# A two-layer hybrid backbone on one core: squared sums and S5 taps in four column tiles, and 14 modulation units moved from the mixers to the routing

## The chip, the cores and the metric

The kernel runs on one core of a Trainium2 chip. The core has five engines, each with its own queue of instructions that it works off strictly in order: TensorE (PE, matrix products), VectorE (DVE), ScalarE (ACT), GpSimd (POOL) and SyncE (SP, which here only issues DMA transfers). They meet through semaphores. The metric is the device time of one execution in microseconds (us), median of several.

## The reference, cut to what matters

The program has two layers. `c` gives six modulation vectors for each layer, four token mixers run on one projection, gates and one output product merge them, and a routed mixture of experts follows.

```
for layer in range(DEPTH):                        # DEPTH = 2
    mod_lat = split(silu(c) @ w_mod[layer] + b_mod[layer], 6)       # w_mod: 1024 x 6144, fp32
    mod_ctx = split(silu(c_ctx) @ w_mod[layer] + b_mod[layer], 6)
    a = modulate(rmsnorm(h, norm1_g), mod[0], mod[1])
    p = split_proj(a @ w_in[layer])
    y_a = deltanet_mixer(...)      # q = l2norm(q), k = l2norm(k): sums of squares over 64 values
    y_b = s5_mixer(...)            # state space; d_skip * u is added
    y_c = diff_attention(...)
    y_d = gla_mixer(...)
    h = h + mod[2] * merge_branches(a, (y_a, y_b, y_c, y_d), w_branch, w_gate, b_gate, w_out)
    f = modulate(rmsnorm(h, norm2_g), mod[3], mod[4])
    h = h + mod[5] * moe_ffn(f, w_router, b_router, w_e_gate, w_e_up, w_e_down)
return rmsnorm(h_lat, final_g)
```

768 tokens (256 of context, 512 latent) go through layer 0, the 512 latent ones alone are needed behind layer 1. There are 16 experts of 1024 x 512 with two chosen for each token.

## The kernel before, in words

**Order.** The code is written stage by stage, but a list scheduler sets the order in which instructions stand in each engine's queue: it simulates all of them with a cost for each and lets whichever can start go ahead. The order is fixed at build time. What the chip does with it is that every engine takes the next instruction of its queue and waits for it, even if a later one could run.

**Modulation.** `mods` (L1317) makes one unit of 256 columns: two loads `w` of 512 KB on SP from three buffers (`MB = 3`), eight products `mod` (L1330, each two passes in the trace) whose weights are two columns (`c` and `c_ctx`), put in four column tiles of the array, then four additions on DVE (L1334) that sum the tiles on top of the bias `bm`, and a store to `md` in DRAM. A layer has 24 units. Eight units of layer 0 are made in front of its first norm; the other 40 (16 of layer 0, 24 of layer 1) are taken one after another from the list `todo` by `some(n)` within layer 0's mixers: 12 ahead of the first DeltaNet pair, 14 ahead of the second, 14 behind it (`MODS = (12, 14)`).

**DeltaNet.** `dn_pair` works on two of four heads. Its squared norms `dn_n` are 12 products (24 passes) with the squared values as 128 x 128 weights and a two-column mask `blk2` as the moving side. There are four calls, two in each layer.

**S5.** `s5_tables` makes in two halves the tables of a layer: powers and products `W`, `O` on DVE and POOL, products `s_w`, and the taps `s_h` (L1088), 16 products (32 passes) in each half with 32-column weights `Bd`, all into PSUM partitions 0 to 31. The taps `H` go by DRAM (`hd`) into the table `td`. Layer 1's tables are made at the end of layer 0's mixers: they reuse the space of layer 0's S5 mixer (whose last products are `s_g`), begin with the load of `sp` (L960), and the merge stands behind them.

**Gates and merge.** The gate products `pg` of the mixers (1536 of them, split precision: `wh`, `wl` are made on ACT and by DVE or POOL at L1289 and L1290) fill PE between the mixers' own steps. The merge begins with `pb<-yh,wh`.

**Routing and experts.** `route` is a generator: up to its `yield` it makes positions (`pos`), one-hots (`hot`) and the first block's tokens; behind it the counts (`cnt`) and the order of the remaining blocks. `moe` then runs 128-token blocks: transpose `pt`, products `pg` (gate and up), transpose `ph`, products `pd` (down). Expert weights come as `raw` loads of 1 MB on SP, are split into `hi` (ACT, L2203) and `lo` (DVE or POOL, L2205).

Of the kernel before, what the change touches and what calls it, by code (L numbers as in the profile page):

```python
# [17 lines left out]
NT = 6  # L18
# [9 lines left out]
PRI = (None, None)  # L28
PRG = (None, None)
PVM = 64  # L30
MODS = (12, 14)
MB = 3
RAW = (3, 5)
RAW2 = (2, 1)
# [7 lines left out]
def const_blob():  # L42
    p = np.arange(128)
    k, i = p[:, None], p[None, :]
    same = (k // 64) == (i // 64)
    j64, i64 = (p % 64)[:, None], np.arange(64)[None, :]
    t = np.arange(512)
    inv = (np.float32(10000.0) ** (-np.arange(8, dtype=np.float32) / np.float32(8))).astype(np.float32)
    ang = np.concatenate([(t // 64).astype(np.float32)[:, None] * inv, (t % 64).astype(np.float32)[:, None] * inv], -1)
    rope = [f(ang).astype(np.float32).reshape(4, 128, 16).transpose(1, 0, 2).reshape(128, 64) for f in (np.cos, np.sin)]  # L50
    parts = dict(
        id=(k == i), id64=(j64 == i64), trif=same & (k <= i), trib=same & (k >= i), blk=same,
        cm0=(k < 64) & (i >= 0), cm1=(k >= 64) & (i >= 0),
        mskf=i64 >= j64, mskb=i64 <= j64, blk2=(k // 64) == np.arange(2)[None, :],
        cos=rope[0], sin=rope[1],
        gmf=(i >= k) * np.float32(32 ** -0.5), gmb=(i <= k) * np.float32(32 ** -0.5),
        id16=(k % 16 == np.arange(16)[None, :]) * 1.0,
        stri=(k < i), one=(k >= 0) & (i >= 0),
        tok=p[:, None] + 128 * np.arange(6)[None, :], exp=np.arange(16)[None, :] * 768 + 0 * k,
        num1=np.arange(1, 16)[None, :] + 0 * k, num16=np.arange(16)[None, :] + 0 * k,  # L60
        iota=i + 0 * k,
    )
    off, cols, c = {}, [], 0
    for n, a in parts.items():
        a = np.ascontiguousarray(a).astype(np.float32)
        off[n] = (c, a.shape[1])
        c += a.shape[1]
        cols.append(a)
    return np.concatenate(cols, 1), off

PRM = (("lre", 16), ("lim", 16), ("ldt", 16), ("bin", 256), ("ct", 512), ("dsk", 8),
       ("g1", 8), ("bm1", 16), ("cc", 16), ("bgt", 32), ("convw", 30), ("dng", 64), ("dtb", 8), ("na", 8),
       ("wg", 256), ("bg", 2), ("glag", 64), ("lv", 128), ("dag", 64), ("glub", 2), ("wr", 128), ("br", 16), ("g2c", 8))
PRO = {n: (sum(m for _, m in PRM[:i]), m) for i, (n, m) in enumerate(PRM)}
# [6 lines left out]
def lay_out(x):  # L83

    a = {n: np.asarray(x[n], dtype=np.float32) for n in x}
    o = {}
    prm = np.zeros((2, 128, NPRM), np.float32)

    def put(l, nm, v):
        c, n = PRO[nm]  # L90
        v = np.asarray(v).reshape(-1, n)
        prm[l, 0:v.shape[0], c:c + n] = v
# [8 lines left out]
    for l in range(2):  # L101
        for nm, src in (("lre", "s5_a_re"), ("lim", "s5_a_im")):
# [2 lines left out]
        put(l, "bin", np.stack([a[n][l].reshape(8, 128, 16).transpose(1, 0, 2) for n in ("s5_b_re", "s5_b_im")], 1))  # L105
        put(l, "ct", np.stack([a[n][l].reshape(2, 8, 2, 16, 64).transpose(2, 4, 0, 1, 3).reshape(128, 2, 128)
                               for n in ("s5_c_re", "s5_c_im")], 2))
        put(l, "dsk", a["s5_d"][l].reshape(8, 32).T)
# [151 lines left out]
def tcol(t):  # L260

    return 128 * t + (4 if t >= 2 else 0)
# [95 lines left out]
def dn_pair(K, l, pr, S, qT, kT, vT, o_out, need):  # L358
# [3 lines left out]
    nc, p, sm = K.nc, K.dn, K.dn_sm  # L362
    idm = K.c("id")
# [10 lines left out]
    sq = [s3([128, 772], "sq") for _ in range(2)]  # L374
    nc.scalar.activation(sq[0], qT, AF.Square)
    nc.scalar.activation(sq[1], kT, AF.Square)
    pn = K.psm("dn_n")
    pnv = pn[:, 0:24].rearrange("p (s t h) -> p s t h", s=2, t=NT)
    for s in range(2):
        for t in range(NT):  # L380
            nc.tensor.matmul(pnv[:, s, t, :], sq[s][:, tcol(t):tcol(t) + 128], K.c("blk2"), start=True, stop=True)
    n2 = sm.tile([128, 24], F32, tag="n2", name="n2")
    nc.vector.tensor_scalar(n2, pn[:, 0:24], 0.25, 1e-6, op0=OP.mult, op1=OP.add)
    rr = rsqrt_(nc, sm, n2, [128, 24], "nr")
    rq = sm.tile([128, NT, 2], F32, tag="rq", bufs=2, name="rq")
    nc.vector.tensor_scalar(rq.rearrange("p t h -> p (t h)"), rr[:, 0:12], 0.125 * 0.5, None, op0=OP.mult)
# [16 lines left out]
    for src, dst, isk in ((kT, Kt, True), (vT, Rv, False)):  # L403
        for t0, n in ((0, 4), (4, 2)):
# [4 lines left out]
            pv = pt[:, 0:n * 128].rearrange("p (a e) -> p a e", e=64)  # L409
# [11 lines left out]
    for cp in range(2):  # L421
        src = bass.AP(tensor=gd.tensor, offset=gd.offset + pr * 24 * 128 + cp * 64, ap=[[0, 64], [128, 24], [1, 64]])
# [41 lines left out]
    for c in range(31):  # L464
        n, m = 31 - c, c + 1
# [101 lines left out]
    for s0, s1 in ((0, 8), (1, 9), (8, 11), (9, 11)):  # L567
# [4 lines left out]
        pv = pb.rearrange("p (s c) -> p s c", c=128)  # L572
# [378 lines left out]
def s5_params(K, l):  # L951
# [4 lines left out]
    def t16(nm):  # L956
        return q.tile([128, 16], F32, tag=nm, name=nm)

    sp = q.tile([128, 824], F32, tag="sp", name="sp")
# [52 lines left out]
    dsk = sp[0:32, 816:824]  # L1012

    rot = q.tile([128, 2, 7, 16], F32, tag="rot", name="rot")
    wr, wi = cs, sn
# [14 lines left out]
def s5_tables(K, l, P, h, td):  # L1030
# [45 lines left out]
    for b in range(2):  # L1076
        r = slice(64 * b, 64 * b + 64)
        for c in range(2):
            G.tensor_copy(Bd[r, c, :, :, 16 * b:16 * b + 16], bb[r, c, :, H4, :])
    H = s4([32, 4, 15, 16], "H")  # L1080
    pss = [K.psmt("s5_h") for _ in range(2)]
    for g in range(4):
        a, o = g // 2, (g % 2) * 256
        for d in range(2):
            lo = 0 if d == 0 else 1
            c0 = o + (128 if d == 0 else 0)
            for c in range(2):
                nc.tensor.matmul(pss[a][0:32, c0:c0 + 128], Bd[:, c, d, g], O[d][:, c, g, lo:lo + 8].rearrange("p e c -> p (e c)"),  # L1088
                                 start=(c == 0), stop=(c == 1))
    for a in range(2):  # L1090
        pv = pss[a][0:32].rearrange("p (g s n) -> p g s n", g=2, s=2)
        Ha = H[:, 2 * a:2 * a + 2]
        nc.scalar.activation(Ha[:, :, 0:8].rearrange("p g n c -> p g (n c)"), pv[:, :, 0], AF.Copy)
        nc.scalar.activation(Ha[:, :, 8:15].rearrange("p g n c -> p g (n c)"), pv[:, :, 1, 16:128], AF.Copy)
        V.tensor_add(Ha[:, :, 7], Ha[:, :, 7], pv[:, :, 1, 0:16])
    dd = p.tile([32, 4, 16], F32, tag="dd", name="dd")
    V.tensor_mul(dd, P["dsk"][:, H4, None].to_broadcast([32, 4, 16]), K.c("id16")[0:32, None, :].to_broadcast([32, 4, 16]))
    V.tensor_add(H[:, :, 7], H[:, :, 7], dd)
    hd = K.dram.tile([32, 4, 240], F32, tag="s5h", bufs=2, name="hd")
    nc.sync.dma_start(hd[:], H.rearrange("p g n c -> p g (n c)"))  # L1100
    cz = sum(n for _, n in S5_TAB[0:4])
    for j in range(8):
        src = hd[:, :, 16 * (7 - j):16 * (7 - j) + 128].rearrange("(b c) g k -> c g b k", b=2)
# [386 lines left out]
def mixers(K, l, md, hold, tile_of, yd, gd, tds):  # L1490
# [91 lines left out]

    if l == 0:
        pm = Hold(tc, "mod1", "left")
        todo = iter([(0, u) for u in range(8, 24)] + [(1, u) for u in range(24)])

        def some(n):
            for _ in range(n):
                i, u = next(todo)
                mods(K, i, md[i], [u], pm, MB, K.psmb)  # L1590

        some(MODS[0])
# [31 lines left out]


    if l == 0:
        some(40 - MODS[0] - MODS[1])
        pm.close()

    def sink_tm(dst, c0, n):  # L1630
# [330 lines left out]
    V.tensor_add(R.tot[:, t0:t1], sel[:, 0], sel[:, 1])  # L1961


def route(K, l, lg, R):

# [385 lines left out]
def backbone(nc, tc, I, out, off):  # L2353
# [37 lines left out]
    for l in range(2):  # L2391
# [30 lines left out]
        routing = route(K, l, lg, R)  # L2422
        next(routing)
        nh = pm[0]
        hs = {}
# [46 lines left out]
```

## Time and profile before

| | |
|---|---|
| median of 3 runs | 2811.99 us (2797.94 to 2814.32) |
| profiled execution | 2812.61 us, of it 2810.6 us span on the core |
| mean granted TensorE clock | 0.908 of full speed |
| PE busy over the span | 2443.4 us (87%) |
| DVE, ACT, POOL busy | 1870.6, 1218.6, 1178.3 us (67, 43, 42%) |

The span runs from the core's first to its last instruction. Busy time is an average over stages with different limits, so the stages are looked at one by one. Layer 0's mixers lie between 118 and 945 us, its merge runs to 1110, its routing from 1110 to 1186 and its experts to about 1530. A PEclk of 1.00 is 2.4 GHz and 0.50 is 1.2 GHz.

### The profile page before, as it was taken

Reading aid. Unit: us, or ns where it says so; the run is one execution under the profiler, and the core shown is the slowest. Engines: PE = TensorE matmul, PEld = TensorE weight load, DVE = VectorE, ACT = ScalarE, POOL = GpSimd, SP = SyncE. Lnnn points to the kernel's source line nnn. Section 1 sums busy time; section 2 is a strip of 40 time slices with the busy share of each in tenths; the row PEclk is TensorE's granted clock in tenths of the full one; section 3 lists DMA queues with packets and bytes.
Section 4 is the critical chain, followed back from the end, with each engine's and each line's share of the span. In section 5 each row is a group of like instructions: output and inputs, shape, how many; then the busy total and the mean of one; then the engine's idle time right before and its main releaser. Section 6 shows DMA issues by size and latency. Waiting matters only on the chain. (4 is left out here: it accounts for less than half of the span.)

```text
span 2810.6 us, 46335 instructions
## 1 busy us (share of the span) xinstructions
PE 2443.4 (87%) x17539; PEld 1974.6 (70%) x17539; DVE 1870.6 (67%) x3515; ACT 1218.6 (43%) x1889; POOL 1178.3 (42%) x854
## 2 busy tenths in 40 slices
PE   6789998899998788599998499989998886699993
PEld 5567687777776676478887388977776665478782
DVE  5968639545659765877775744665584576787775
ACT  4121232365443322366665323244655432366672
POOL 2701205522417453466664320155343043576763
PEclk9889999999988999699999699989998598799996
DMA  7488832414322775478887553343432184588884
GB/s 295 163 260 287 263 91 74 145 58 143 113 82 95 266 228 201 178 271 307 305 306 253 209 186 116 100 130 120 113 102 62 57 263 170 196 335 298 305 309 160
DMA packets 227896, 534.95 MB, mean 190 GB/s; under 512 B 85478, under 2 KB 108230, under 8 KB 202054
## 3 DMA queue, kind: packets, MB, share of 16 engines
q1 hardware_dynamic: 216710, 510.81, 53.5%
q0 software_dynamic: 10944, 20.99, 2.1%
q8 instruction: 142, 2.33, 0.3%
q14 instruction: 100, 0.82, 0.1%
HBM read 452.33 MB, written 100.35 MB: 197 GB/s over the span
## 5 line engine op out<-in xcount | busy, mean ns | idle before, releaser
L2205 DVE TENSOR_TENSOR lo<-raw,hi 128x2048 fp32r<-128x2048 f32 x124 | 418.2, 3381 | 106.3 <-ACT hi L2203 106.1
L2203 ACT ACTIVATE hi<-raw 128x2048 fp32r<-128x2048 f32 x192 | 364.2, 1913 | 79.3 <-issue 34.8
L2205 POOL TENSOR_TENSOR lo<-raw,hi 128x2048 fp32r<-128x2048 f32 x68 | 335.9, 4941 | 142.0 <-ACT hi L2203 127.5
L1290 POOL TENSOR_TENSOR wl<-wr,wh 128x512 fp32r<-128x512 f32 x128 | 185.0, 1449 | 295.5 <-ACT wh L1289 276.2
L1301 PE MATMUL pg<-ah,wl 128*128 128x512 f32 (+1 forms) x768 | 286.4, 374 | 7.1 <-POOL wl L1290 7.1
L1299 PE MATMUL pg<-ah,wh 128*128 128x512 f32 (+1 forms) x768 | 286.8, 374 | 5.8 <-ACT wh L1289 3.7
L1300 PE MATMUL pg<-al,wh 128*128 128x512 f32 (+1 forms) x768 | 286.4, 373 | 0.0
L1300 PE MATMUL pg<-lo,xh 128*128 128x512 f32 x608 | 244.9, 403 | 13.8 <-DVE lo L2205 11.0
L1299 PE MATMUL pg<-hi,xh 128*128 128x512 f32 x608 | 243.8, 404 | 5.4 <-ACT xh L2230 4.0
L1301 PE MATMUL pg<-hi,xl 128*128 128x512 f32 x608 | 243.0, 401 | 0.0
L1289 ACT ACTIVATE wh<-wr 128x512 fp32r<-128x512 f32 (+3 forms) x208 | 147.8, 715 | 206.9 <-PE pg L1300 66.8
L1301 PEld LDWEIGHTS pg<-ah,wl 128*128 128x128 f32 x768 | 151.9, 198 | 31.1 <-POOL wl L1290 8.0
L1299 PEld LDWEIGHTS pg<-ah,wh 128*128 128x128 f32 x768 | 152.1, 198 | 28.7 <-ACT wh L1289 4.2
L1300 PEld LDWEIGHTS pg<-al,wh 128*128 128x128 f32 x768 | 152.0, 198 | 22.8 <-issue 0.2
L1300 PE MATMUL pt<-wl,ah 128*128 128x256 f32 (+1 forms) x544 | 159.0, 293 | 2.2 <-DVE wl L1290 2.2
L1299 PE MATMUL pt<-wh,ah 128*128 128x256 f32 (+1 forms) x544 | 158.4, 292 | 2.3 <-ACT zst L1578 2.3
L1301 PE MATMUL pt<-wh,al 128*128 128x256 f32 (+1 forms) x544 | 157.6, 290 | 0.0
L870 DVE TENSOR_REDUCE nm<-da_m 128x1 f32<-128x384 f32 (+1 forms) x144 | 76.2, 539 | 120.0 <-PE da_m L869 118.9
L1300 PEld LDWEIGHTS pg<-lo,xh 128*128 128x128 f32 x608 | 116.9, 192 | 42.0 <-DVE lo L2205 14.4
L1299 PEld LDWEIGHTS pg<-hi,xh 128*128 128x128 f32 x608 | 117.2, 193 | 29.9 <-ACT xh L2230 5.1
L1301 PEld LDWEIGHTS pg<-hi,xl 128*128 128x128 f32 x608 | 116.8, 192 | 23.2
L1299 PE MATMUL pd<-hi,hh 128*128 128x512 f32 x304 | 120.6, 397 | 7.3 <-ACT hh L2257 4.2
(735 smaller groups left out, 6172.1 us busy)
## 6 DMA issues: line engine op xcount, KB each, us to landing
raw<-in_w_e_gate SPq DMA_DIRECT2D x64, 1024.0 KB
raw<-in_w_e_up SPq DMA_DIRECT2D x64, 1024.0 KB
raw<-in_w_e_down SPq DMA_DIRECT2D x64, 1024.0 KB
w<-in_wm SPq DMA_DIRECT2D x80, 512.0 KB
wr<-in_w_gate SPq DMA_DIRECT2D x128, 256.0 KB
wr<-in_win SPq DMA_DIRECT2D x40, 512.0 KB
gd<-gst SPq DMA_DIRECT2D x32, 384.0 KB
g<-gd SPq DMA_DIRECT2D x32, 384.0 KB
```

The lines of the kernel that those rows point to most:

```text
L870: nc.vector.tensor_reduce(nm[:, g, m, qt:qt + 1], ps[:, 0:k1 - k0], axis=AX.X, op=OP.max, negate=True)
L1289: nc.scalar.activation(h, r, AF.Copy)
L1290: (nc.gpsimd if pool_lo else nc.vector).tensor_sub(l, r, h.bitcast(F32))
L1299: nc.tensor.matmul(out, ah, bh, start=(i == 0), stop=False)
L1300: nc.tensor.matmul(out, ah, bl, start=False, stop=False)
L1301: nc.tensor.matmul(out, al, bh, start=False, stop=(i == n - 1))
L2203: nc.scalar.activation(h, r, AF.Copy)
L2205: (nc.gpsimd if (j % 3 == 2 if pool_lo is None else pool_lo) else nc.vector).tensor_sub(l_, r, h.bitcast(F32))
```

## The change

Three parts. In the DeltaNet norms the mask becomes the weights (32 columns, `blk32`) and the squared values the moving side, in four column tiles; a copy on ACT, three transposes and one smaller DVE operation bring the sums back. In the S5 taps the four groups of a half go to four column tiles, which leaves two copies and two DVE operations where there were four and four. Of the 40 modulation units 26 stay in the mixers (12, 12 and 2) and 14 are made in `route`, called ahead of its `yield` in the first layer, with three `w` buffers of their own and two PSUM buffers `fill` of the routing's pool.

```diff
-MODS = (12, 14)
+MODS = (12, 12, 2)
...
     pn = K.psm("dn_n")
-    pnv = pn[:, 0:24].rearrange("p (s t h) -> p s t h", s=2, t=NT)
-    for s in range(2):
-        for t in range(NT):
-            nc.tensor.matmul(pnv[:, s, t, :], sq[s][:, tcol(t):tcol(t) + 128], K.c("blk2"), start=True, stop=True)
+    for x in range(3):
+        for c in range(4):
+            a = tcol(3 * (c % 2) + x)
+            nc.tensor.matmul(pn[32 * c:32 * c + 32, 128 * x:128 * x + 128], K.c("blk32"), sq[c // 2][:, a:a + 128],
+                             start=True, stop=True)
+    ns = s3([128, 384], "ns")
+    nc.scalar.activation(ns, pn[:, 0:384], AF.Copy, scale=0.25)
+    pn = K.psm("dn_n")
+    for x in range(3):
+        nc.tensor.transpose(pn[:, 128 * x:128 * x + 128], ns[:, 128 * x:128 * x + 128], idm)
     n2 = sm.tile([128, 24], F32, tag="n2", name="n2")
-    nc.vector.tensor_scalar(n2, pn[:, 0:24], 0.25, 1e-6, op0=OP.mult, op1=OP.add)
+    nc.vector.tensor_scalar(n2.rearrange("p (c x h) -> p c x h", c=4, x=3),
+                            pn[:, 0:384].rearrange("p (x c e) -> p c x e", x=3, c=4)[:, :, :, 0:2], 1e-6, None, op0=OP.add)
...
-    H = s4([32, 4, 15, 16], "H")
-    pss = [K.psmt("s5_h") for _ in range(2)]
-    for g in range(4):
-        a, o = g // 2, (g % 2) * 256
-        for d in range(2):
...
+    H = s4([128, 15, 16], "H")
+    ps = K.psmt("s5_h")
+    for d in range(2):
+        lo, c0 = d, 128 * (1 - d)
+        for c in range(2):
+            for g in range(4):
+                nc.tensor.matmul(ps[32 * g:32 * g + 32, c0:c0 + 128], Bd[:, c, d, g], O[d][:, c, g, lo:lo + 8].rearrange("p e c -> p (e c)"),
                                  start=(c == 0), stop=(c == 1))
...
-        todo = iter([(0, u) for u in range(8, 24)] + [(1, u) for u in range(24)])
+        todo = iter([(0, u) for u in range(8, 20)] + [(1, u) for u in range(14)])
...
-        some(40 - MODS[0] - MODS[1])
+        some(MODS[2])
...
     G.tensor_add(all_, pre[:, n - 1], tot[:, n - 1])
+    fill(lambda nm: pp.tile([128, 512], F32, tag="fill", bufs=2, name=nm))
     pp.close()
     p.close()
     yield
...
+        def fill(psm):
+            if l == 0:
+                pf = Hold(tc, "mod2", "left")
+                for i, u in [(0, u) for u in range(20, 24)] + [(1, u) for u in range(14, 24)]:
+                    mods(K, i, md[i], [u], pf, MB, psm)
+                pf.close()
```

What stands in the queues moves at two places. On PE, at the end of layer 0's mixers, where layer 1's tables (`s_w`, `s_h`) are made and the merge (`pb`) begins, this stood before:

```order
L910 MATMUL da_s<-st 128x512
L1058 MATMUL s_w<-cb,W 128x128 x4
L1300 MATMUL pg<-al,wh 128x256
...
L1088 MATMUL s_h<-O,Bd 32x128 x16
...
L1465 MATMUL yT<-cb,o 128x128 x6
...
L1300 MATMUL pg<-al,wh 128x512
L1301 MATMUL pg<-ah,wl 128x512
L1299 MATMUL pb<-yh,wh 128x256
```

and this stands there now:

```order
L1065 MATMUL s_w<-cb,W 128x128 x4
L1299 MATMUL pg<-ah,wh 128x512
L1300 MATMUL pg<-al,wh 128x512
L1301 MATMUL pg<-ah,wl 128x512
L1093 MATMUL s_h<-O,Bd 32x128 x8
L1465 MATMUL yT<-cb,o 128x128 x6
L1065 MATMUL s_w<-cb,W 128x128 x4
L1093 MATMUL s_h<-O,Bd 32x128 x8
L1065 MATMUL s_w<-cb,W 128x128 x12
L1093 MATMUL s_h<-O,Bd 32x128 x16
L1299 MATMUL pb<-yh,wh 128x256
```

The gate products have moved forward: ahead of the last `s_g` of layer 0 stand 1348 of them rather than 1151 (of the difference of 197, 97 are 512 columns wide and 100 are 256) and 449 products of the differential attention rather than 418; between the first `s_w` and `pb` stand 34 gate products rather than 219, and none at all behind the first `s_h`.

On PE at layer 0's routing, where `pos` begins the routing's own products and `pt` the first expert block, this stood before:

```order
L1869 MATMUL pq<-sel,lt 128x16 x2
L2004 MATMUL pos<-seltot,cb 128x96
L2007 MATMUL pos<-pre,cb 128x96
L2020 MATMUL ent<-v_12110,hot 128x2 x6
L2051 MATMUL wt<-w_12138,hot 128x1 x6
L2091 MATMUL cnt<-all,cb 128x16
L2228 MATMUL pt<-cb,x 128x128 x4
L1299 MATMUL pg<-hi,xh 128x512
```

and this stands there now:

```order
L1869 MATMUL pq<-sel,lt 128x16 x2
L1330 MATMUL mod<-w,sc 2x256 x28
L2004 MATMUL pos<-seltot,cb 128x96
L2007 MATMUL pos<-pre,cb 128x96
L1330 MATMUL mod<-w,sc 2x256 x4
L2020 MATMUL ent<-v_11818,hot 128x2 x6
L1330 MATMUL mod<-w,sc 2x256 x8
L2051 MATMUL wt<-w_11846,hot 128x1 x6
L1330 MATMUL mod<-w,sc 2x256 x72
L2229 MATMUL pt<-cb,x 128x128 x4
L2092 MATMUL cnt<-all,cb 128x16
L1299 MATMUL pg<-hi,xh 128x512
```

All 112 products of the 14 units stand ahead of the first expert block, 84 of them behind `pos`.

On SP, whose queue issues the loads at the same place, this stood before (`iota` is the routing's first load, `h1d` and `fd` its last stores):

```order
L1992 DMA iota<-in_blob 128x128
L2200 DMA raw<-in_w_e_up 128x2048
L2200 DMA raw<-in_w_e_down 128x2048
L1844 DMA h1d_86<-h 128x1024
L1890 DMA fd_87<-h 128x1024 x2
L2200 DMA raw<-in_w_e_down 128x2048
```

and this stands there now:

```order
L1992 DMA iota<-in_blob 128x128
L1325 DMA w<-in_wm 128x1024 x2
L1332 DMA bm<-in_b_mod 2x256
L1844 DMA h1d_86<-h 128x1024
L1325 DMA w<-in_wm 128x1024
L1332 DMA bm<-in_b_mod 2x256
L1890 DMA fd_87<-h 128x1024
L1325 DMA w<-in_wm 128x1024
L1890 DMA fd_87<-h 128x1024
L1325 DMA w<-in_wm 128x1024 x2
L1335 DMA md_67<-bm 2x256
```

The rest of the 28 loads `w` follows, with three `raw` loads among them; the second half of the first block's `up` weights, which stood right behind `iota`, and its second `down` load stand behind the last store of the units.

## Rows read from the trace of the kernel before

**Rows 1.** Windows of the mixers: stretch, length, busy us (instructions) per engine, PEclk, DMA, GB/s.

```profile
200.00:350.00 150.00, 139.62 (x1778) 105.09 (x1775) 112.29 (x236) 33.63 (x62) 26.43 (x19) 0.96 0.86 272
400.00:650.00 250.00, 234.00 (x2180) 194.84 (x2178) 143.53 (x300) 113.71 (x243) 97.69 (x85) 0.94 0.33 95
...
850.00:900.00 50.00, 42.30 (x304) 34.59 (x303) 50.00 (x157) 17.85 (x35) 34.01 (x28) 0.90 0.27 93
900.00:950.00 50.00, 35.95 (x181) 29.65 (x180) 35.84 (x105) 12.60 (x24) 31.91 (x54) 0.84 0.67 233
```

**Rows 2.** The modulation's products among the groups of PE in 118 to 400 us.

```profile
L1330 PE MATMUL mod<-w,sc 128*2 128x256 f32 x640 | 53.7, 411 | 22.5 <-DMA w<-in_wm 21.4 <-DVE R L939 1.0
```

**Rows 3.** Instructions of the tile `mod`: ns min/median/max, first and last start.

```profile
L1330 PE MATMUL mod<-w,sc x640: 376/378/634, 124.6 to 356.9; 128*2 128x256 f32 x160
L1334 DVE TENSOR_TENSOR bm<-mod,bm x160: 402/417/427, 130.3 to 362.0; 2x256 f32<-2x256 f32 x160
```

**Rows 4.** Instructions of the lines of the DeltaNet norms and the S5 taps.

```profile
L381 PEld LDWEIGHTS dn_n<-cb,sq x96: 186/192/238, 192.8 to 2029.0; 128*128 128x128 f32 x96
L381 PE MATMUL dn_n<-cb,sq x96: 165/251/298, 192.9 to 2029.0; 128*128 128x2 f32 x96
...
L1088 PEld LDWEIGHTS s_h<-O,Bd x128: 106/110/177, 91.7 to 921.4; 128*32 128x32 f32 x128
L1088 PE MATMUL s_h<-O,Bd x128: 272/273/422, 91.7 to 921.5; 128*32 128x128 f32 x128
```

**Rows 5.** Timeline of SP and PE, end of the mixers: start, us, instruction.

```profile
829.46 0.47 SPq L960 DMA_DIRECT2D sp<-in_prm  x1
...
918.94 2.81 PE L1088 MATMUL s_h<-O,Bd 128*32 128x128 f32 x24 [1.23 <-DVE O L1071]
948.70 0.58 PE L1299 MATMUL pb<-yh,wh 128*128 128x256 f32 x1 [2.76 <-ACT wh L1289]
```

**Rows 6.** Groups of DVE in 829 to 935 and of POOL in 829 to 945 us.

```profile
L916 DVE SCALAR_TENSOR_TENSOR pe<-pe,nlam 128x512 f32<-128x512 f32 (+1 forms) x8 | 7.5, 935 | 0.0
L1290 POOL TENSOR_TENSOR wl<-wr,wh 128x512 fp32r<-128x512 f32 x13 | 21.1, 1626 | 22.3 <-ACT wh L1289 20.0 <-issue 2.4
```

**Rows 7.** Timeline of SP at the routing.

```profile
1111.35 0.33 SPq L1992 DMA_DIRECT2D iota<-in_blob  x1
...
1124.98 1.08 SPq L1890 DMA_DIRECT2D fd<-h  x2
```

**Rows 8.** Timeline of PE at the routing.

```profile
1133.42 0.74 PE L2004 MATMUL pos<-seltot,cb 128*128 128x96 f32 x2 [15.80 <-DVE seltot L1961]
...
1151.51 1.11 PE L2228 MATMUL pt<-cb,x 128*128 128x128 f32 x4 [5.67 <-DMA x<-fd,tokfirst]
...
1174.92 0.39 PE L1301 MATMUL pg<-hi,xl 128*128 128x512 f32 x1
...
1186.01 0.77 PE L1299 MATMUL pd<-hi,hh 128*128 128x512 f32 x1 [0.82 <-DVE wtranked L2071]
```

**Rows 9.** Windows of the modulation loads, the routing and the experts; columns as in rows 1.

```profile
160.00:340.00 180.00, 169.62 (x1919) 125.46 (x1921) 137.10 (x289) 48.76 (x86) 24.11 (x19) 0.96 0.84 271
1150.00:1160.00 10.00, 2.76 (x7) 1.54 (x7) 10.00 (x5) 0.60 (x1) 10.00 (x3) 0.50 0.71 268
1240.00:1300.00 60.00, 60.00 (x284) 49.59 (x284) 42.74 (x27) 41.82 (x37) 39.84 (x16) 1.00 0.80 296
```

**Rows 10.** Timeline of DVE and of POOL at the routing.

```profile
1134.09 4.43 DVE L2039 TENSOR_TENSOR ws<-w 128x6 f32<-128x6 f32 x1
1147.98 4.27 DVE L2096 TENSOR_SCALAR over<-cnt 128x14 f32<-128x14 f32 x1
1152.17 0.15 DVE L2137 TENSOR_SCALAR c<-cnt 1x16 f32<-1x16 f32 x1
...
1133.98 4.52 POOL L2205 TENSOR_TENSOR lo<-raw,hi 128x2048 fp32r<-128x2048 f32 x1
1146.63 14.54 POOL L2205 TENSOR_TENSOR lo<-raw,hi 128x2048 fp32r<-128x2048 f32 x3
```

More of the change, by code (lines that the diff above doesn't have):

```diff
@@ L53, in const_blob @@
         cm0=(k < 64) & (i >= 0), cm1=(k >= 64) & (i >= 0),
-        mskf=i64 >= j64, mskb=i64 <= j64, blk2=(k // 64) == np.arange(2)[None, :],
+        mskf=i64 >= j64, mskb=i64 <= j64, blk32=(k // 64) == np.arange(32)[None, :],
         cos=rope[0], sin=rope[1],
@@ L69, in const_blob @@
     return np.concatenate(cols, 1), off
-PRM = (("lre", 16), ("lim", 16), ("ldt", 16), ("bin", 256), ("ct", 512), ("dsk", 8),
+PRM = (("lre", 16), ("lim", 16), ("ldt", 16), ("bin", 256), ("ct", 512), ("dsk", 2),
        ("g1", 8), ("bm1", 16), ("cc", 16), ("bgt", 32), ("convw", 30), ("dng", 64), ("dtb", 8), ("na", 8),
@@ L107, in lay_out @@
                                for n in ("s5_c_re", "s5_c_im")], 2))
-        put(l, "dsk", a["s5_d"][l].reshape(8, 32).T)
+        put(l, "dsk", a["s5_d"][l].reshape(2, 128).T)
         put(l, "g1", cm(a["norm1_g"][l]))
@@ L957, in t16 @@
         return q.tile([128, 16], F32, tag=nm, name=nm)
-    sp = q.tile([128, 824], F32, tag="sp", name="sp")
+    sp = q.tile([128, 818], F32, tag="sp", name="sp")
     nc.sync.dma_start(sp, prm(K, l, "lre", "dsk"))
@@ L1011, in s5_params @@
     ct = sp[:, 304:816].rearrange("p (d c g i) -> p d c g i", d=2, c=2, g=8)
-    dsk = sp[0:32, 816:824]
+    dsk = sp[:, 816:818]
     rot = q.tile([128, 2, 7, 16], F32, tag="rot", name="rot")
@@ L1079, in s5_tables @@
             G.tensor_copy(Bd[r, c, :, :, 16 * b:16 * b + 16], bb[r, c, :, H4, :])
-    H = s4([32, 4, 15, 16], "H")
-    pss = [K.psmt("s5_h") for _ in range(2)]
-    for g in range(4):
-        a, o = g // 2, (g % 2) * 256
-        for d in range(2):
[L1085 to L1088, printed above, removed]
-                                 start=(c == 0), stop=(c == 1))
@@ L1090, in s5_tables @@
[L1090 to L1097, printed above, removed]
@@ L1098, in s5_tables @@
-    V.tensor_add(H[:, :, 7], H[:, :, 7], dd)
-    hd = K.dram.tile([32, 4, 240], F32, tag="s5h", bufs=2, name="hd")
-    nc.sync.dma_start(hd[:], H.rearrange("p g n c -> p g (n c)"))
+    H = s4([128, 15, 16], "H")
[5 more added lines that the diff above has]
+                nc.tensor.matmul(ps[32 * g:32 * g + 32, c0:c0 + 128], Bd[:, c, d, g], O[d][:, c, g, lo:lo + 8].rearrange("p e c -> p (e c)"),
+                                 start=(c == 0), stop=(c == 1))
@@ L1101, in s5_tables @@
+    nc.scalar.activation(H[:, 0:8].rearrange("p n c -> p (n c)"), ps[:, 0:128], AF.Copy)
+    nc.scalar.activation(H[:, 8:15].rearrange("p n c -> p (n c)"), ps[:, 144:256], AF.Copy)
+    V.tensor_add(H[:, 7], H[:, 7], ps[:, 128:144])
+    V.scalar_tensor_tensor(H[:, 7], K.c("id16"), P["dsk"][:, h:h + 1], H[:, 7], op0=OP.mult, op1=OP.add)
+    hd = K.dram.tile([128, 240], F32, tag="s5h", bufs=2, name="hd")
+    nc.sync.dma_start(hd[:], H.rearrange("p n c -> p (n c)"))
     cz = sum(n for _, n in S5_TAB[0:4])
@@ L1102, in s5_tables @@
     for j in range(8):
-        src = hd[:, :, 16 * (7 - j):16 * (7 - j) + 128].rearrange("(b c) g k -> c g b k", b=2)
+        src = hd[:, 16 * (7 - j):16 * (7 - j) + 128].rearrange("(g b c) k -> c g b k", g=4, b=2)
         dst = td[16 * j:16 * j + 16, cz:cz + 1024].rearrange("c (g b k) -> c g b k", g=4, b=2)
@@ L1961, in choose, with route @@
     V.tensor_add(R.tot[:, t0:t1], sel[:, 0], sel[:, 1])
-def route(K, l, lg, R):
+def route(K, l, lg, R, fill):
     nc, tc, I = K.nc, K.tc, K.I
@@ L2421, in backbone @@
         R.ent = rk.tile([128, 2, NT - 2 * l, 4], I32, name="ent")
-        routing = route(K, l, lg, R)
+        def fill(psm):
[4 more added lines that the diff above has]
+                pf.close()
+        routing = route(K, l, lg, R, fill)
         next(routing)
```

## The prediction

> **What bounds the kernel now.** I read the windows by stage first, then the groups of the moved work, then the timelines around the two places where the queues change. In layer 0's mixers PE is busy for 139.62 of 150 us while the modulation units are made and for 234.00 of 250 behind them [rows 1], so work taken off PE there should come back, unless another chain sets the end. At the end it does: from 850 to 900 us DVE is busy for 50.00 of 50 and PE for 42.30, from 900 to 950 PE for 35.95 [rows 1]. There layer 1's S5 tables are made, from the load of `sp` at 829.46 to the last taps at 918.94 + 2.81 = 921.75, and the merge begins at 948.70 [rows 5]. Layer 0's routing is bound neither by PE nor by DMA alone: PE waits 15.80 us for `seltot` [rows 8], has 2.76 busy us of 10 at a granted clock of 0.50, the 1.2 GHz level, and DVE and POOL are both full [rows 9]. So PE has room there, DVE has little. Behind it the experts keep PE busy for 60.00 of 60 us at a clock of 1.00 [rows 9]: whatever the first block loses is lost at the end too.
>
> **The mixers, what is taken away.** The 40 units cost PE 53.7 us, and 21.4 us went in waits for their `w` loads [rows 2]. One unit is 53.7 / 40 = 1.34 us, 14 are 18.8. Of the waits I give them their share, 14/40 of 21.4 = 7 us (bounds 0 and 21). A call of the norms is 24 weight loads of 0.192 us, 4.6 us; the new weights have 32 columns like those of the taps, whose load takes 0.110 [rows 4], which gives 2.6, from which three transposes and a copy on ACT, whose result DVE waits for, take a part back: 1 us a call, 2 for layer 0 (bounds -2 and +5 for both, the old cost halved or the new steps all on the chain). In sum 18.8 + 7 + 2 = 28 us of PE time.
>
> A norm product with 2 moving columns takes 251 ns and a tap product with 128 takes 273 [rows 4], so the moving side, 64 times longer now, costs nearly nothing. A rule speaks against the change there: the Trainium skill, TensorEngine Tiling (Array Packing), Tiling Modes, says that a change of the tiling mode drains the engine. By an estimate from that rule, one product of 251 ns lost going in and one coming out, the four norm calls and four tap halves would pay 8 x 0.5 = 4 us and their gain would be gone; no row here shows a drain by itself.
>
> **The mixers, what is put in its place.** The order has moved the gates forward. Ahead of layer 0's last `s_g` stand 97 more gate products of 512 columns, 100 of 256 and 31 more of the differential attention. The experts show 284 products in 60.00 us, 0.211 us each [rows 9], so these are 97 x 0.211 + 100 x 0.106 + 31 x 0.13 = 20.5 + 10.6 + 4.0 = 35 us (the halves are estimates by width). S5's mixer then ends at -28 + 35 = +7 us. The load of `sp` follows it directly, and the tables behind it are DVE's. They can only become shorter: within them DVE has 7.5 us of the attention's `pe` and POOL 21.1 us of the gates' `wl` [rows 6], nearly all of which is done earlier now, since 34 gate products are left rather than 219. Bounds are 0 and 7.5 + 21.1 = 29; I take half, 14, because POOL is not the chain's only engine. So the merge begins at +7 - 14 = **-7 us**. PE's gates no longer cover the tables: the time that PE saved is spent waiting for taps. Range: -28 if the whole saving passes through, +7 if the tables are not shorter. The merge itself I cost at nothing; its products and loads are the same.
>
> **The routing.** The 112 `mod` products stand on PE ahead of `pt`, so the first block begins behind the last unit, at a time T. Three routes give T.
> By bytes: `iota` is at 1111.35 and the second `fd` at 1124.98 [rows 7]; `fd` waits for POOL and DVE, and on SP all but three or four of the 28 loads wait behind it. About 25 loads of 0.52 MB and three `raw` of 1.05 MB are 16 MB; at 271 GB/s, the rate in the mixers [rows 9], this is 60 us, T = 1185.
> By the units' own pace: before, 40 of them ran from 124.6 to 356.9 [rows 3], 5.8 us each with three buffers; 14 from 1111 on give 1111 + 81 = 1192.
> By PE: 14 x 1.34 = 18.8 us at a clock of 1.00, up to twice that at 0.50, which fits under the loads.
> DVE's 56 additions are 56 x 0.417 = 23 us [rows 3], put in among the routing's chain. That chain is held where POOL runs: `ws` of six columns takes 4.43 us beside a `lo` of 4.52, `over` 4.27 within the three `lo` of 14.54 [rows 10]. Additions queued behind such an operation wait with it, and their PSUM buffers are two, so PE waits then too: up to two holds, 9 us. I take **T = 1188**, bounds 1183 and 1200.
>
> On these holds the trace shows a pattern: `over`, on 128 partitions, takes 4.27 us, the copy `c` right behind it 0.15 [rows 10]. The Trainium skill, GPSIMD Engine Reference, Specifications, says that GpSimd shares its SBUF interfaces with VectorE and contends with those of its instructions that use two ports or have two SBUF inputs. By that rule the additions themselves, with one input in PSUM, would pass; the result by this rule alone would be T = 1185 and 3 us less in the sum. Rows 3 cannot decide it, their maximum of 427 ns has little of POOL beside it.
>
> From T to the first `pd`: before, from the first `pt` at 1151.51 to `pd` at 1186.01 [rows 8] were 34.5 us with waits; without them the 48 gate and up products, the transposes and the step from the last `pg` (1174.92) to `pd` (11 us, [rows 8]) come to some 17 us, 22 if the second `up` load, issued only behind the last store, is late with its split (1.05 MB are 3.9 us at 271 GB/s, and POOL's `lo` takes 4.52, [rows 10]). Taken 19: `pd` at 1188 + 19 = 1207, against 1186.01: **+21 us**, range 1183 + 17 - 1186 = +14 to 1200 + 22 - 1186 = +36. The experts pass it on in full.
>
> **Layer 1 and the taps.** Two norm calls at 1 us, and taps on the path: the last 24 passes take 2.81 us [rows 5], at best a quarter in four tiles, with two DVE operations fewer. Together -3 us, bounds -8 and +2.
>
> **The sum** is -7 + 21 - 3 = +11 us. The profiled execution took 2812.61 us, 0.6 above the median, so both give **2823 us**.
>
> **The rivals.**
> 1. *The mixers keep all that PE saves.* PE is the fullest engine there [rows 1], and if the tables shrink by the whole 29 us, the merge begins 28 us earlier or so. Against it: DVE is at 50.00 of 50 in the tables with little of the rest. With +21 at the routing and -3: 2803; with the routing's +14 as well, 2796. Only if the routing also hides its units (rival 3) is it 2780, faster by more than 1%.
> 2. *The units hold the experts back longer* (slower than before). SP is one queue: a store of `md` that waits for DVE's additions stands ahead of the next `w`, and DVE's additions stand behind the held routing operations. If each unit behind `pos` (1133.42, [rows 8]) takes the pace of before (5.8 us) plus two holds, 10.5 units end at 1133.4 + 61 + 9 = 1203, and with the late `up` load `pd` is at 1225, +39; with S5's chain at +7, the sum is +43, 2855. With the late load it passes 1% from T = 1188 on if the chain is at +7 (+7 + 24 - 3), from T = 1202 with the forecast's -7. For it: DVE is full and the queues are strict. Against it: the pace of before was set by the mixers' other work as much as by the buffers.
> 3. *The routing hides the units.* Before, PE waited 5.67 us for the first block's tokens [rows 8], and DVE's chain was held until POOL's three `lo` ended at 1161 [rows 10]; both would now run beside the units. If T is 1172 and DVE's chain is then out of the way, the routing costs +5: -7 + 5 - 3 gives 2807. Against it: 16 MB do not load by 1172 at any rate shown in rows 9.
> 4. *The tiles do not run side by side.* Norms and taps then cost as before or more: +5 on the forecast, 2828, no case of its own in the chances.
>
> **How the numbers follow.** About 1%, 28 us, is what a measurement of this kernel tells from no change (the three runs lie 16 us apart). Forecast 0.42, rival 1 0.23, rival 2 0.17, rival 3 0.18. The forecast and rival 3 lie within 1%, so does rival 1 but for its meeting with rival 3 and a larger share of waits (0.10 to 0.13); rival 2 is beyond it at nearly all its times. Faster 0.13, same 0.70, slower 0.17. For 8 in 10 the range leaves out the low end of rival 1 and the high end of rival 2: 2793 to 2850. The predicted time is the forecast's, 2823.
>
> **What would show it.** The merge's first `pb` near 942 with PE idle ahead of the taps in 830 to 920; the `sp` load a few us later than 829; the last `mod` product at 1183 to 1200 and the first `pd` at about 1207; PE full in the experts, ending some 11 us later. Wrong would be: `pb` before 925 (rival 1), a last `mod` product behind 1200 (rival 2) or before 1175 (rival 3).

## The result, and the profile after

| | before | after |
|---|---|---|
| median | 2811.77 us, 4 runs | 2849.97 us, 4 runs (2837.60 to 2856.82) |
| ratio | | 1.0141, 95% interval 1.0091 to 1.0191 |
| profiled execution, span | 2812.61, 2810.6 us | 2853.99, 2852.2 us |
| mean granted TensorE clock | 0.908 | 0.901 |

The change costs 38 us where 11 were forecast: the sign was right, the size was not, and the time lies at the very end of the range. To see what one trace is worth, each kernel was profiled a second time (the last two experiments). These are the milestones on PE in us, in all four traces:

| from, to | before | before again | after | after again | mean change | forecast |
|---|---|---|---|---|---|---|
| start to first `dn_n` | 193 | 200 | 199 | 191 | -1 | 0 |
| to the merge's first `pb` | 756 | 755 | 756 | 749 | -2 | -7 |
| to `pos` | 185 | 185 | 188 | 187 | +3 | } +21 |
| to the first `pd` | 53 | 53 | 86 | 91 | +36 | } |
| layer 0's experts, to their last `pd` | 352 | 352 | 353 | 352 | +1 | 0 |
| to layer 1's first `pb` | 706 | 695 | 699 | 699 | -1 | } -3 |
| to the last `pd` | 525 | 522 | 528 | 528 | +4 | } |

So the loss lies in one place, between `pos` and the first `pd`. I follow the prediction's steps there. The windows of the mixers and the experts after (columns as in rows 1):

```profile
200.00:350.00 150.00, 140.66 (x1760) 117.56 (x1753) 102.20 (x206) 38.69 (x71) 26.22 (x19) 0.99 0.68 202
400.00:650.00 250.00, 231.74 (x2092) 192.32 (x2091) 155.82 (x322) 109.71 (x245) 104.11 (x86) 0.91 0.32 91
850.00:900.00 50.00, 44.02 (x320) 36.71 (x318) 46.36 (x172) 16.55 (x30) 27.38 (x24) 0.93 0.27 95
900.00:950.00 50.00, 7.83 (x64) 4.26 (x64) 43.00 (x174) 5.46 (x12) 34.78 (x53) 0.51 0.51 170
```

From 900 to 950 us PE is busy for 7.83 us at the 1.2 GHz level, where it had 35.95 [rows 1]: the gates no longer cover the tables, as forecast. The group of the `mod` products in 118 to 400 us, the lines of the norms and the taps, and then (from the timelines of SP and PE) the end of the mixers:

```profile
L1330 PE MATMUL mod<-w,sc 128*2 128x256 f32 x416 | 35.8, 422 | 16.9 <-DMA w<-in_wm 11.1 <-DVE R L954 5.3 <-DVE B L473 0.3
```

```profile
L381 PEld LDWEIGHTS dn_n<-sq,cb x96: 106/110/111, 199.0 to 2089.7; 128*32 128x32 f32 x96
L381 PE MATMUL dn_n<-sq,cb x96: 272/273/298, 199.0 to 2089.8; 128*32 128x128 f32 x96
...
L1093 PE MATMUL s_h<-O,Bd x128: 272/421/424, 99.1 to 931.0; 128*32 128x128 f32 x128
```

```profile
850.15 0.42 SPq L967 DMA_DIRECT2D sp<-in_prm  x1
...
929.16 2.27 PE L1093 MATMUL s_h<-O,Bd 128*32 128x128 f32 x32
955.57 0.58 PE L1299 MATMUL pb<-yh,wh 128*128 128x256 f32 x1 [24.14 <-ACT wh L1289]
```

The units left in the mixers cost 35.8 us and 11.1 of waits, against 53.7 and 21.4 [rows 2]: 17.9 and 10.3 us less, where 18.8 and 7 were forecast. The `sp` load comes 20.7 us later than before [rows 5], the last taps some 10 us later, and `pb` 7: the tables took back two thirds of it.

PE at the routing, and SP there:

```profile
1143.41 0.74 PE L2004 MATMUL pos<-seltot,cb 128*128 128x96 f32 x2 [0.39 <-DVE seltot L1961]
...
1196.69 1.89 PE L1330 MATMUL mod<-w,sc 128*2 128x256 f32 x16 [3.83 <-DVE bm L1334]
1198.51 1.12 PE L2229 MATMUL pt<-cb,x 128*128 128x128 f32 x4
...
1215.57 0.39 PE L1301 MATMUL pg<-hi,xl 128*128 128x512 f32 x1
...
1227.87 1.11 PE L2257 MATMUL ph<-cb,hd 128*128 128x128 f32 x4 [8.98 <-DVE hd L2247]
1229.67 0.79 PE L1299 MATMUL pd<-hi,hh 128*128 128x512 f32 x1 [0.69 <-ACT hh L2258]
```

```profile
1117.69 0.33 SPq L1992 DMA_DIRECT2D iota<-in_blob  x1
...
1132.35 0.73 SPq L1890 DMA_DIRECT2D fd<-h  x1
...
1201.31 0.36 SPq L2201 DMA_DIRECT2D raw<-in_w_e_up  x1
```

The last `mod` product ends at T = 1198.6, 80.9 us behind `iota`, where the forecast has 1188 - 1111.35 = 76.7 [rows 7]. From T to the last `pg` of the first block are 17 us, but `pd` follows only 31 us behind T, because `ph` waits 8.98 us for DVE's `hd`. In the kernel before it waited 1.02:

```profile
1177.86 0.65 PE L2256 MATMUL ph<-cb,hd 128*128 128x128 f32 x4 [1.02 <-DVE hd L2246]
```

DVE and POOL around these 31 us:

```profile
1194.42 3.58 DVE L1334 TENSOR_TENSOR bm<-mod,bm 2x256 f32<-2x256 f32 x8 [6.74 <-DMA bm<-in_b_mod]
1199.17 1.77 DVE L1334 TENSOR_TENSOR bm<-mod,bm 2x256 f32<-2x256 f32 x4 [1.18 <-DMA bm<-in_b_mod]
...
1201.06 0.17 DVE L2094 COPY cnt<-cnt 128x16 f32<-128x16 f32 x1
...
1208.13 2.29 DVE L2206 TENSOR_TENSOR lo<-raw,hi 128x2048 fp32r<-128x2048 f32 x1 [0.84 <-ACT hi L2204]
...
1220.30 0.67 DVE L2246 SCALAR_TENSOR_TENSOR hd<-hd,pg 128x512 f32<-128x512 f32 x1
...
1221.40 3.55 DVE L2161 SCALAR_TENSOR_TENSOR ova<-ovb,ova 1x192 f32<-1x192 f32 x1
1224.88 0.14 DVE L2024 TENSOR_SCALAR pr<-ent 128x4 f32<-128x4 f32 x1
1224.95 2.27 DVE L2206 TENSOR_TENSOR lo<-raw,hi 128x2048 fp32r<-128x2048 f32 x1
1227.15 0.67 DVE L2247 TENSOR_TENSOR hd<-hd,pg 128x512 f32<-128x512 f32 x1
```

```profile
1212.46 19.15 POOL L2206 TENSOR_TENSOR lo<-raw,hi 128x2048 fp32r<-128x2048 f32 x2 [4.99 <-ACT hi L2204]
```

`cnt` starts the routing's chain of small DVE operations. Before, `over`, its second step, was at 1147.98 [rows 10], ahead of the first `pt`; now the chain begins 2.5 us behind T. The second half of the first block's `up` weights is loaded at 1201.31, behind the last store of the units, and its split with those of `down` puts four `lo` of 2.3 us ahead of the first `hd` and a fifth ahead of the second; `ova`, one of many rows of 0.34 us, takes 3.55 here, within the time of POOL's two `lo`, in which other rows of its form take 0.34 as well.

The last unit's products wait 3.83 us for additions of DVE, and these wait 6.74 us for a bias load `bm`, which stands on SP's one queue behind the stores `md` and loads `w` of other units. The additions themselves are not drawn out: the longest of the 160 takes 427 ns, as before [rows 3].

### The profile page after: what moved, and what is told of

The parts are those of the page before. It is cut to its first block, busy times and chain, and to the rows that moved or that the text cites. A ratio compares the mean times of both kernels' runs of the same rounds, so it can differ in the third digit from the quotient of the medians.

```text
span 2852.2 us, 46349 instructions
## 1 busy us (share of the span) xinstructions
PE 2426.7 (85%) x17551; PEld 1948.1 (68%) x17551; DVE 1872.5 (66%) x3507; ACT 1214.9 (43%) x1885; POOL 1193.8 (42%) x854
## 5 line engine op out<-in xcount | busy, mean ns | idle before, releaser
L1300 PE MATMUL pc<-al,wh 128*128 128x256 f32 (+3 forms) x352 | 123.4, 351 | 2.4 <-DVE al L1404 1.6
```

Of the source, the lines that this page charges most:

```text
L1300: nc.tensor.matmul(out, ah, bl, start=False, stop=False)
```

## The experiments

The kernel before was run beside each, and each ratio is to those runs. Two theories stood against each other at the start: that the 14 units beside the routing cost what is missing, or that the new order of the queues does, wherever the work lies.

**One part of the change alone.** The tiles alone, all 40 units left in the mixers:

```diff
-MODS = (12, 12, 2)
+MODS = (12, 14)
-        todo = iter([(0, u) for u in range(8, 20)] + [(1, u) for u in range(14)])
+        todo = iter([(0, u) for u in range(8, 24)] + [(1, u) for u in range(24)])
```

> The norms and taps in column tiles, all 40 modulation units left in the mixers. Theory 1 (all of the loss comes from the 14 moved units): 2804 to 2813 us, the first merge product within 5 us of 948.7, first pd of layer 0 within 8 us of 1186. Theory 2 (the column tiles, by the engine's change of tiling mode or by the order they bring, make the mixers longer): 2818 to 2830 us, the merge's first product at 955 or later.

2854.86 us, ratio 1.0175 (1.0136 to 1.0213). That is a loss as large as the whole change's, without a unit beside the routing. In its trace `pos` to `pd` take 53 us as before; the loss lies in layer 1, whose code is that of the changed kernel: its mixers take 724 us there and 699 in the changed kernel. The units moved alone, norms and taps as before:

> The 14 units moved to the routing, norms and taps as before. Theory 1: 2846 to 2860 us, first pd of layer 0 at 1225 to 1240. Theory 2: 2830 to 2840 us, since the mixers would keep their 7 us.

2898.60 us, 1.0333 (1.0295 to 1.0370). The parts cost 48 and 92 us, both together 38: they do not add up, so what one such run costs is not the price of its edit. The norms alone, and the taps alone:

> The kernel before with the new norms alone. Theory E (the norms' chain now passes PE's queue twice, and the transposes stand behind gate products, 18 us in the second pair of the changed kernel): the time from the first dn_n product to the n operation is 8 us or more in at least one of four calls, 2815 to 2850 us. Theory F (norms are neutral): 2800 to 2812 us.

> The kernel before with the new taps alone. Theory E: 2800 to 2812 us, the taps behind the last table operation 2 us shorter. Theory F (the taps' tiles or the order they bring cost the 48 us of both together): 2840 us or more.

2868.84 us, 1.0203 (1.0150 to 1.0256), and 2813.66 us, 1.0007 (0.9979 to 1.0036). With the taps alone the first `pd` lies 998 us behind the first `dn_n`, against 993 and 992, and nothing is lost or gained.

**The order by itself.** The kernel before without the 14 units (only their bias is loaded and stored, so their products, sums and weight loads are left out):

```diff
-                    mods(K, i, md[i], [u], pf, MB, psm)
+                    bias(K, i, md[i], u, pf)
```

> The kernel before without the 14 units (their columns are the bias alone), norms and taps as before: the mixers have the PE time back and nothing is paid for it. Theory A (PE's time in the mixers is not what ends them: waits and the clock take its place): 2800 to 2820 us. Theory B (the mixers would be faster, but the column tiles ate it in the changed kernel): 2775 to 2792 us, the merge's first product before 930.

2859.35 us, 1.0204 (1.0127 to 1.0281): strictly less work, and 45 us more. This settles that a new order alone can cost as much as the change did. It does not yet say that it did so here. For that the same was left out of the changed kernel, whose PE order stays that of the changed kernel up to the merge and in layer 1, but for a row in thousands:

> The changed kernel without the 14 units: their columns of the modulation are the bias alone, with no weight loads, products or additions. The order of PE up to the merge is that of the changed kernel. Theory 1 (the units beside the routing hold the experts back): the routing is as before, so what is left is the mixers' +7 and layer 1's -2: 2810 to 2820 us, first pd at about 1193. Theory 3 (the experts start late because the order of the routing is worse, not because of the units): 2835 to 2850 us.

2816.26 us (10 runs), 1.0020 (0.9993 to 1.0047). With the order of the changed kernel and no unit beside the routing the loss is gone. By the medians, each against the kernel before run beside it, the units cost 38 - 9 = 29 us, and order, tiles and mixers together +9 or less, an amount that the interval does not tell from nothing. PE in that trace:

```profile
1135.38 0.74 PE L2010 MATMUL pos<-seltot,cb 128*128 128x96 f32 x2 [15.92 <-DVE seltot L1967]
...
1184.40 0.66 PE L2263 MATMUL ph<-cb,hd 128*128 128x128 f32 x4
1185.74 0.79 PE L1299 MATMUL pd<-hi,hh 128*128 128x512 f32 x1 [0.69 <-ACT hh L2264]
```

From `pos` to `pd` are 50 us, as before (53), and `ph` does not wait. Measured to the end of layer 0's experts, from `pos` on, it is 407 us here, 404 in both traces before, 439 and 443 in the changed kernel. So in one order the units cost that stretch 32 to 36 us. (The columns that are the bias alone act behind layer 0's routing; the stretch behind layer 1's first `pb` still takes 530 us, against 528.)

**What sets T, and what the step behind it.** Seven units there, 33 in the mixers:

> Seven units beside the routing and 33 in the mixers. Theory 1, a price for each unit (T moves by 14 units in about 75 us, 5.4 us each, so by 37 us for seven, until the routing's own chain ends last): first pd at 1190 to 1200, 2813 to 2828 us. Theory 4, a fixed price (the first block's loads and splits come behind whatever units there are): first pd at 1210 to 1220, 2833 to 2842 us.

2845.90 us, 1.0138 (1.0085 to 1.0191). T lies 22 us behind `pos` rather than 55, `pd` 60 rather than 86, and the step from T to `pd` is 37: it does not shrink with the units. Neither theory met its times. Yet from `pos` to the end of the experts it is 408 us, 4 more than before: seven units are nearly free there. What makes the total no better lies elsewhere: 763 us from the first `dn_n` to `pb` (756 in the changed kernel), where seven units more are made, and 536 behind layer 1's first `pb` (528), in another order. In all eight traces with units beside the routing the experts end 378 to 388 us behind T, wherever T lies, 22 to 65 us behind `pos`: there the place of T sets the price. One sum on DVE for each unit instead of four (`ct=1`, 14 additions rather than 56):

> The changed kernel with the 14 units beside the routing made in one column tile: eight products summed in PSUM and one addition on DVE instead of four (14 instead of 56). Theory C (the loads set the end of the units): last mod product within 5 us of 1198, first pd within 6 us of 1230, 2840 to 2856 us. Theory D (DVE's queue sets it): last mod product 10 to 20 us earlier, 2825 to 2840 us.

2882.04 us, 1.0229 (1.0166 to 1.0291). From the first `mod` to T are 80 us, against 75, and the first `pd` is at 1245: neither expectation was met. The run does not part the two theories, because the eight products of a unit, now in one column tile, no longer run side by side: those of the 14 units take PE 57 us rather than 27. All 14 units from the same two loads, so 26 loads are left out; the modulation of layer 1 is another one and one more pass of experts runs at the end, so that the total does not compare:

> The changed kernel in which the 14 units beside the routing use the two loads of the first of them, 26 loads of 512 KB fewer (the columns of 13 units are therefore others); products, additions and stores stay. Theory C (the loads set the end of the units): last mod product within 30 us of pos rather than 55, first pd within 62 us of pos rather than 86, 2818 to 2832 us. Theory D (the queues of PE and DVE set it): last mod product still 45 us or more behind pos, 2840 us or more.

```profile
1163.93 1.89 PE L1343 MATMUL mod<-w,sc 128*2 128x256 f32 x16 [6.84 <-DVE bm L1347]
...
1196.35 1.11 PE L2270 MATMUL ph<-cb,hd 128*128 128x128 f32 x4 [8.45 <-DVE hd L2260]
1198.15 0.79 PE L1299 MATMUL pd<-hi,hh 128*128 128x512 f32 x1 [0.69 <-ACT hh L2271]
```

2920.83 us. T lies 33 us behind `pos` rather than 55, between the two expectations: the 26 loads are worth 22 us of T, and 21 to 25 of the 32 to 36 us up to the end of the experts (418 us from `pos`). They do not set T alone. From the first `mod` on the units still take 57 us, and what ends T here is the additions, which wait for the small bias loads:

```profile
1160.88 3.34 DVE L1347 TENSOR_TENSOR bm<-mod,bm 2x256 f32<-2x256 f32 x8 [7.10 <-DMA bm<-in_b_mod]
```

No run takes these away. The step behind T is 32 us again, with 8.45 of wait for `hd`. So it hangs on what stands behind T in the queues, not on the loads `w` before it. To part the two things on DVE there, the routing's counts (from `cnt` to the ranks, and the additional blocks' numbers up to `ova`) were written ahead of the units:

```diff
+    ps2 = pp.tile([128, 512], F32, name="cnt")
+    nc.tensor.matmul(ps2[:, 0:16], K.c("one"), all_, start=True, stop=True)
...
     fill(lambda nm: pp.tile([128, 512], F32, tag="fill", bufs=2, name=nm))
     pp.close()
...
-    ps2 = R.psum("cnt")
-    nc.tensor.matmul(ps2[:, 0:16], K.c("one"), all_, start=True, stop=True)
```

> The changed kernel with the routing's counts (cnt, over, the ranks and the additional blocks' numbers ova, ovb) written ahead of the 14 units instead of behind them. PE's order is the same up to the routing; there cnt stands behind the 32nd mod product. If the first block waits because the routing's chain on DVE begins only behind the last unit: the last mod product stays about 55 us behind pos, but some 25 small operations and the held ova are gone from DVE between it and ph, so that the step from the last mod product to the first pd is 23 to 27 us rather than 31 to 36, and layer 0's experts begin 6 to 9 us earlier against pos. If the late second half of up and its splits on DVE and POOL set it alone: the step stays at 31 to 36 and ph still waits 8 to 9 us for hd. In both cases the total is that of the changed kernel less what the step loses, 2838 to 2850, but for layer 1's mixers, whose order is another one and may move it by 20 us either way.

```profile
1200.68 2.20 PE L1330 MATMUL mod<-w,sc 128*2 128x256 f32 x16 [1.90 <-DMA w<-in_wm]
...
1215.71 1.09 PE L2229 MATMUL pt<-cb,x 128*128 128x128 f32 x4 [5.25 <-DVE xl L2232]
...
1233.23 0.60 PE L2257 MATMUL ph<-cb,hd 128*128 128x128 f32 x4
```

2869.15 us, 1.0203 (1.0141 to 1.0265). Neither expectation met the step as such: `pd` is again 36 us behind T, but `ph` waits no more, and 41 gate and up products of the second block stand in the queue ahead of the first `pd`. The measure that holds for both orders is the end of layer 0's experts, 378 us behind T here and 382 to 388 in the other seven traces with units there (384 and 388 in the changed kernel). So the chain behind the last unit costs some 5 to 11 us of that stretch, by one trace. The rest stays: PE still waits 5.25 us for `xl`, which stands on DVE behind a `lo` of the late `up` half. T itself is 65 us behind `pos` here, so that from `pos` to the end of the experts it is 442 us, no less than in the changed kernel: moved ahead of the units, the chain delays them. Layer 1's mixers take 727 us on top.

**Units elsewhere.** Behind the first block's products, with one `w` buffer:

> The changed kernel with the 14 units written behind the first expert block instead of beside the routing, with one weight buffer and in the experts' PSUM tile. Theory 1 (the units cost what they hold back in front of the first block): pos to first pd is 50 to 58 us as before (87 in the changed kernel), and the experts, full on PE, take the units' 19 us: 2826 to 2842 us. Theory I (the units cost the same wherever they stand, since the first blocks wait for their loads either way): 2845 us or more.

2926.09 us, 1.0439 (1.0411 to 1.0468). The first `pd` comes 49 us behind `pos`, as without the units, but the second one only at 1342: the units stand in PE's queue between the next blocks and hold each of them. In the tables at the end of the mixers, where PE idles, one sum for each, and with the scheduler told to prefer the second DeltaNet pair and S5 (next experiment):

> The kernel before with the 14 units behind S5's table code at the end of layer 0's mixers (one column tile, one addition each) and with the same preference; norms and taps as before, nothing beside the routing. Theory G: the units fill PE where the tables leave it idle, first pb 930 to 946, pos to first pd within 6 us of 53, 2785 to 2808 us. Theory H: the units' additions lengthen DVE's table chain, first pb at 950 or later, 2812 us or more.

2904.60 us, 1.0392 (1.0325 to 1.0459): the `mod` products run from 927 to 995 us, and `pb` is at 995.

**The chain of the mixers first.** In layer 0 the second DeltaNet pair and S5 are preferred when the order is made, in the changed kernel and in the one before:

```diff
-        s5()
+        with tc.high_priority(None):
+            s5()
```

> The changed kernel with the second DeltaNet pair and S5's mixer of layer 0 preferred in the order: ahead of the last s_g stand 1174 gate products (1151 before, 1348 in the changed kernel), and 47 are left behind the last taps. Theory G (the order with the gates ahead of that chain costs the mixers their time): last s_g at 825 or earlier (847 in the changed kernel, 825 before), first pb 935 to 945, 2822 to 2838 us. Theory H (the place of the gates is not what ends the mixers): last s_g at 838 or later, first pb within 6 us of 956, 2843 to 2858 us. Layer 1's order may add or take some 15 us in either.

> The kernel before with the same preference for the second DeltaNet pair and S5's mixer, as the control for the next and the last but one. Theory G: 2790 to 2812 us, last s_g at 815 or earlier, first pb within 8 us of 949. Theory H: 2805 to 2825 us.

2884.67 us, 1.0280 (1.0254 to 1.0306), and 2844.90 us, 1.0142 (1.0096 to 1.0188). In the changed kernel `s_g` ends at 796 us rather than 847, and still the merge:

```profile
944.47 0.58 PE L1299 MATMUL pb<-yh,wh 128*128 128x256 f32 x1 [9.69 <-ACT wh L1289]
```

52 us of head start on S5 bring 11 at the merge (4 against the second trace of the changed kernel): from the last `s_g` to `pb` are 149 us now instead of 108, since the gates that were put off stand there again. And layer 1's mixers, whose code has no preference, take 753 us (740 in the kernel before with it) against 695 to 706 in the four traces above: the order of later work changes with that of earlier work. Over all kernels that stretch took 683 to 773 us; in the four traces with the changed kernel's order of PE in it (the changed kernel twice, without the units, and with two loads) it took 699 to 714.

**Both kernels once more.**

> The kernel before once more, for the spread of a stage from run to run: if the first merge product lies within 8 us of 948.7 and layer 1's mixers within 10 us of 705, the changed kernel's +7 at the merge is not chance alone; if they move by 15 us or more, it cannot be told from chance in one trace.

> The changed kernel once more, for the same: pos to first pd within 4 us of 87 if the routing's loss is fixed by the queues; first merge product within 8 us of 955.6.

2805.76 and 2842.77 us; their milestones are in the table above.

## Why the prediction came out as it did

**The mixers: right, as far as the spread lets it be told.** Forecast -7, measured -2 as the mean of two traces each; 743 to 761 us from the first `dn_n` to `pb` in seven traces of that order, against 756 and 755. S5's end came 3 to 21 us later in them, 13 on average (forecast +7), and the stretch from there to `pb` took 108 us instead of 123, -15 (forecast -14). Rival 1 is refuted: nothing near 28 us came through. (Its meeting with rival 3 was also summed wrongly: -28 + 5 - 3 from 2812.6 is 2787, not 2780, and so not beyond 1%.) One wait that the prediction did not have is seen in the norms. In the second pair the sums are ready early, but the transposes that bring them back stand behind gate products on PE:

```profile
432.42 0.86 PE L381 MATMUL dn_n<-sq,cb 128*32 128x128 f32 x22
...
452.20 0.42 PE L387 MATMUL dn_n<-cb,ns 128*128 128x128 f32 x1
```

That is 19 us inside one call for which I had 1 us. It is not shown to be what holds S5: with the norms alone, in an order of their own, the transposes of that call come 6 us behind their sums and S5's end is 18 us later all the same. Why S5's end was later than +7 stays open.

**The tiles run side by side: rival 4 is refuted.** 22 norm products of 0.273 us stand in 0.86 us. On the rule that I weighed (the Trainium skill, TensorEngine Tiling (Array Packing), Tiling Modes: a change of tiling mode drains the engine) the trace shows no cost near the 0.25 us of that estimate: the next gate product begins at 433.20 us, before the modelled end of the last norm product at 433.28. The taps' median of 421 ns instead of 273 goes with the granted clock of 0.51 in their window; their minimum is 272, and before, in one column tile, their range was 272 to 422 [rows 4].

**T: right, its reason in part.** The forecast of 76.7 us behind `iota` met 80.9. The loads `w` count: two instead of 28 brought T down by 22 us. But the route by bytes had them as the whole of it, and T still lay 33 us behind `pos` without them; the bias loads for which the additions wait were in none of the three routes. So the number was in part luck.

**The step that failed** is "from T to the first `pd`", "some 17 us, ... Taken 19". It measured 31 and 36, and 32 to 39 in six other kernels with units there. It failed twice. The sum itself was wrong: 48 products at the 0.211 us of [rows 9] are 10 us, two transposes 2 and the step behind the last `pg` 11, which is 23 and not 17. And T to the end of the last `pg` took 17 and 18, which makes 28: in the first trace the first eight products start some 0.43 us apart, at a granted clock of 0.50, those behind them 0.23 at 1.00, and 48 passes of `ent` stand among them. And I kept that step at 11 us, its size before, though `cnt` and the splits that had run beside the routing now begin behind the last unit: `ph` waits 8.5 to 9 us for `hd`, and the step took 14 and 18. Leaving the units out of the same order brings all of it back (50 us from `pos` to `pd`), moving the counts ahead of them some 5 to 11 us behind T, which T itself then loses. How much of the remainder is the late `up` half stays open: no run loads it ahead of the units.

**Rival 2** named the right place and sign, and its 2855 is nearer than the forecast; but its mechanism, a T of 1203 (70 us behind `pos`) through held additions, is not what happened: T lay 55 us behind `pos`, and of such holds behind `pos` the trace has one, `ws` with 4.07 us, while the later additions wait for their bias loads. With T right and the step at 31 to 36 the forecast's own sum gives 2835 to 2840; T's 4 us and the 5 that the mixers did not bring make it 2844 to 2849. **Rival 3** is refuted: T was not near 1172.

**Layer 1 and the taps:** -3 forecast, +3 measured, within what one order differs from another by. The taps alone bring nothing that can be measured.

## What to carry to other kernels

Work put into an idle engine ahead of a stage costs that stage not only the time until the last piece of it, but everything that had run beside the idle time and now queues behind it: list what the other engines did in the gap before calling it empty. How much was put there decides: seven units ended early enough to cost the routing and the experts 4 us, fourteen cost them 32 to 36. Where a scheduler sets the order, do not price an edit by leaving it out or adding it alone; compare kernels whose order is the same but for the edit, as here the changed kernel with and without the units. And add up the parts of each step once more from the rows: the slip, the clock and the passes in between were 9 of the 12 to 17 us by which that step failed.

## What was not expected of the hardware

The same kernel starts in two ways. The window from 30 to 60 us (columns as in rows 1), first of the kernel before in its two traces:

```profile
30.00:60.00 30.00, 25.95 (x192) 19.59 (x191) 20.35 (x63) 13.78 (x25) 13.59 (x15) 0.94 0.71 269
```

```profile
30.00:60.00 30.00, 27.20 (x156) 19.00 (x157) 18.73 (x44) 12.72 (x23) 13.76 (x11) 0.66 0.60 229
```

and of the changed kernel:

```profile
30.00:60.00 30.00, 26.28 (x155) 18.57 (x156) 18.34 (x36) 12.87 (x22) 14.69 (x12) 0.66 0.54 205
```

```profile
30.00:60.00 30.00, 26.07 (x192) 19.75 (x193) 20.21 (x63) 14.08 (x25) 13.32 (x14) 0.94 0.70 266
```

The granted clock is 0.94 or 0.66 there, and all that follows comes 7 to 8 us earlier or later. In the four runs of the changed kernel the time goes with the mean granted clock, from 2837.60 us at 0.908 to 2856.82 at 0.900; thirteen runs of the kernel before lie between 2792.22 at 0.919 and 2820.50 at 0.904. So the time of one kernel's runs goes with the granted clock; which causes which is not shown. A single trace of each kernel would have put 6 us of the start on the change. The start does not decide the total: of the two traces of the kernel before, the one with 0.94 there is the longer by 7 us.
